# A chunked recurrence's triangular inverse: block-diagonal 128x128 products replaced by pairs of 64x64 products

## The chip, the core and the metric

One core of a Trainium2 chip runs the whole kernel. The metric is device time in microseconds. The engines are PE (matrix products; PEld is its weight load), DVE (vector), ACT (scalar), POOL (here it issues the gathers by index) and SP (here it issues the other transfers).

## The reference

One layer of a streaming encoder for 512 tokens of 1024 features: attention (8 heads) and an RWKV-7 recurrence (8 heads of 64) side by side, then a product-key expert layer with 16384 experts, of which each of 8 heads takes 16 per token.

```python
x = x + jnp.concatenate([y_a, y_b], axis=-1) @ w_o[l]     # y_a attention, y_b recurrence
x = x + peer_ffn(rms_norm(x, g_ffn[l]), ...)
# the recurrence, per head, one token after the other:
sk = jnp.einsum('bhij,bhj->bhi', state, kk_t)
state = (state * w_t[:, :, None, :] - sk[..., None] * (kk_t * a_t)[:, :, None, :]
         + v_t[..., None] * k_t[:, :, None, :])
y = jnp.einsum('bhij,bhj->bhi', state, r_t)
# the expert layer, per block of 128 tokens, after the best 16 per head are found:
act = jax.nn.gelu(jnp.einsum('thkd,td->thk', expert_u[idx], hb), approximate=False)
return jnp.einsum('thk,thkd->td', gate * act, expert_v[idx])
```

The kernel does the recurrence in chunks of 64 tokens. Within a chunk the dependence of a token on those before it is a unit lower triangular 64x64 system per head, and its inverse is needed.

## The kernel before

The 512 tokens are four blocks of 128, and a block is two chunks. Each block goes through five stages: F (norm and projections), R (`rwkv_chunks`: what the chunks need, the inverse among it), M (attention), S (`rwkv_scan`: the recurrence over chunks, whose state update is L756) and B (output projection L792, norm, search L848 and routing of experts, whose last matmuls are L947). A loop at the end of `layer_kernel` steps the stages' generators in turn, by assumed costs and by which stage needs which, and so sets the order in which the code is emitted; from that the framework's scheduler fixes each engine's order. An engine then runs its own list strictly in order and waits at the instruction whose data isn't there.

The expert layer is done in two ways. The tokens of blocks 0 and 3 gather rows of the expert tables: `experts` issues 512 gathers of 128 rows (L978, on POOL), and each is followed by one DVE pass over 128x1024 (L988 for the first table, L991 for the second). Four buffers `ga` take turns. Blocks 1 and 2 go through all experts on PE (`dense`): activations L1103 and L1117, sums `po` L1138 and L1149, with DVE and ACT splitting operands in two parts (L1064, L1063).

The inverse is made by doubling, in levels 1, 2, 4, 8, 16 and 32, with 8 heads side by side in the columns and the two chunks of the block on the two halves of the partitions. X and Y are the inverse so far and its transpose. Each level multiplies the system with X and masks the result (L674, then L683), and two further products give the next X and Y (L690, L692); L702 is the last product. Each product multiplies both chunks at once: the weights are a 128x128 block-diagonal matrix per head, with one chunk in each diagonal block. The block diagonals are `INT` (the system), `YB` and `TB`; `stacked` (L665) fills the latter two on ACT, one half of the partitions at a time. The trace holds two PE records for each of these float32 products. L642 is an earlier product of the same stage, already in 64x64 pieces in quarters of the array, and L730 is one of the scan in one quarter.

The lanes' PSUM banks are counted in `BANKS`: two for R (lane 1) and two for S (lane 4) before.

Of the kernel before, what the change touches and what calls it, by code (L numbers as in the profile page):

```python
# [35 lines left out]
# columns of the packed per-channel vectors  # L36
# [7 lines left out]
# columns of the packed per-feature rows  # L44
# [6 lines left out]
# candidate pairs (a, b) of the two sorted lists that can be among the best 16 sums, in order of a * 16 + b:  # L51
# (a, b) has (a + 1) * (b + 1) - 1 pairs before it that are at least as large
# [3 lines left out]
# lanes of stages: buffers, banks and weight tiles (count, width) of each  # L56
LANE = {"R": 1, "M": 2, "S": 4, "F": 3, "B": 3}
BANKS = {1: 2, 2: 2, 3: 2, 4: 2}
# [5 lines left out]
# blocks whose tokens gather their experts' rows, blocks that go through all experts  # L64
# [4 lines left out]
# dense blocks: gates of HALF * 128 experts at a time, in GBUFS tiles of SUB * 128; activations run AHEAD tiles ahead,  # L69
# FIRST of them before the first gates, KEPT more wait in DRAM  # L70
# [6 lines left out]
def u_whole(e):  # L77
    """float32 products of four passes, where the vector engine has no time to split; else three exact parts"""
    return e < 28 or 47 <= e - AHEAD < 64
# [7 lines left out]
def layer_kernel(ctx: ExitStack, tc: tile.TileContext, x, pos, cvec, rvec, w_mla, w_rwkv, w_uq, w_ukv, lora, g2,  # L87
# [5 lines left out]
    # what the last block's tail needs lies apart: its pools outlive those of the other stages  # L93
# [4 lines left out]
    # the tail takes over the buffers of the second lane  # L98
# [13 lines left out]
    def bank():  # L112
        cnt[0] += 1
        return psums[lane[0]].tile([P, 512], F32, tag=f"ps{lane[0]}", name=f"ps{cnt[0]}", bufs=BANKS[lane[0]])

# [24 lines left out]
    # ---------------------------------------------------------------- constants  # L140
# [65 lines left out]
    # rows (beta s | kappa s), columns (alpha t | rho t)  # L206
# [3 lines left out]
    predl = cst([P, 2, C], "predl", I32)  # L210
    V.tensor_tensor(predl, upp[:, None, :].to_broadcast([P, 2, C]), bdm, op=OP.mult)
    pred1 = cst([P, C], "pred1", I32)
    V.tensor_copy(pred1, lev1t)
    eyebd = med(2, C)
    V.tensor_tensor(eyebd, eye[:, None, :].to_broadcast([P, 2, C]), bdm, op=OP.mult)
    INT = cst([P, H, 2, C], "INT")
    Y1 = cst([P, H, C], "Y1")
    YB = cst([P, H, 2, C], "YB")
    G.memset(YB, 0.0)
    TB = cst([P, H, 2, C], "TB")  # L220
    G.memset(TB, 0.0)
    V.tensor_copy(INT, eyebd[:, None].to_broadcast([P, H, 2, C]))
    V.tensor_copy(Y1, eye[:, None].to_broadcast([P, H, C]))
# [35 lines left out]
    # rotary tables, token-major  # L259
# [50 lines left out]
    def square_sum(src, scr, acc):  # L310
        """the squares go to a tile that is written after them"""
        act(scr, src, AF.Square, accum_out=acc)

    def head_squares(src, n, acc, h0=0):
        """acc[:, h0 + i] = sum of squares of src[:, i, :n]"""
        for i in range(src.shape[1]):
            act(sb([P, QK], "hscr", dt=BF16)[:, :n], src[:, i, :], AF.Square, accum_out=acc[:, h0 + i:h0 + i + 1])

    # ---------------------------------------------------------------- stages
    def norm_in(xt, hT, carry):  # L320
        """channel-major normalized tokens, after the last one of the block before"""
        ss = sb([P, 1], "ss", 2)
        square_sum(xt.rearrange("p (a b) -> p a b", a=KC), hT[:, :, 1:], ss)
        r = rstd(ss, 1, 1.0 / D, EPS, "nx")
        act(xt, xt, AF.Copy, scale=r)
        if carry is None:
            V.memset(hT[:, :, 0:1], 0.0)
        else:
            V.tensor_copy(hT[:, :, 0:1], carry)
        for i in range(2):  # L330
            p = bank()
            for j in range(4):
                nc.tensor.transpose(p[:, j * P:(j + 1) * P], xt[:, (4 * i + j) * P:(4 * i + j + 1) * P], ident)
            for j in range(4):
                act(hT[:, 4 * i + j, 1:P + 1], p[:, j * P:(j + 1) * P], AF.Copy, scale=col("g_mix", 4 * i + j))
            yield
        carry = sb([P, KC, 1], "carry", 2)
        V.tensor_copy(carry, hT[:, :, P:P + 1])
        return carry

    def rwkv_in(b, hT):
        pm = {}
        if b == EARLY:
            # the gather's buffers are idle until the first block's experts are known
            t = [gb([P, D], "ga", GA).rearrange("p (a b) -> p a b", b=P) for _ in range(2)]
            pm = {"k": t[0][:, 0:4], "r": t[0][:, 4:8], "v": t[1][:, 0:4], "x": t[1][:, 4:6]}
# [14 lines left out]
    def mla(b, hT, yT):  # L361
# [31 lines left out]
        # queries  # L393
# [32 lines left out]
        # keys and values  # L426
# [27 lines left out]
        # block-causal attention, four heads at a time  # L454
# [73 lines left out]
    def rwkv_chunks(b, pm):  # L528
# [68 lines left out]
        # bonus weight and gate  # L597
# [8 lines left out]
        # values, token-major  # L606
# [17 lines left out]
        # chunk-local products  # L624
# [12 lines left out]
        # inverse of the unit lower triangular systems: two chunks stacked on the partitions, heads side by side  # L637
        for s in range(2):
            p = bank()
            for j in range(4):  # L640
                for c in range(2):
                    mm(p[c * C:(c + 1) * C, j * C:(j + 1) * C], BK[s * C:(s + 1) * C, j, c, 0, :],  # L642
                       AR[s * C:(s + 1) * C, j, c, 0, :], start=True, stop=True)
            p3 = p[:, :4 * C].rearrange("p (a b) -> p a b", a=4)
            V.copy_predicated(INT[:, s::2], predl[:, None].to_broadcast([P, 4, 2, C]),
                              p3[:, :, None, :].to_broadcast([P, 4, 2, C]))
            V.copy_predicated(Y1[:, s::2], bm(pred1, 4), p3)
            yield
# [13 lines left out]
        def stacked(t, y):  # L662
            for c in range(2):
                q = slice(c * C, (c + 1) * C)
                act(t[q, :, c, :], y[q], AF.Copy)  # L665
# [3 lines left out]
        Y, Yb = Y1, stacked(YB, Y1)  # L669
        X = None  # L670
        for lv in LEVELS:
            t1 = bank()
            for h in range(H):
                mm(t1[:, h * C:(h + 1) * C], INT[:, h].rearrange("p a b -> p (a b)"), eye if X is None else X[:, h, :],  # L674
                   start=True, stop=True)
            t13 = t1.rearrange("p (a b) -> p a b", a=H)
            if lv == 1:
                X = med(H, C)
                V.tensor_tensor(X, t13, bm(lmask[1], H), op=OP.mult)
                yield  # L680
                continue
            t1s = med(H, C)
            V.tensor_tensor(t1s, t13, bm(lmask[lv], H), op=OP.mult)  # L683
            t1b = stacked(TB, t1s)
            if lv == LEVELS[-1]:
                break
            yield
            xp, yp = bank(), bank()
            for h in range(H):
                mm(xp[:, h * C:(h + 1) * C], Yb[:, h].rearrange("p a b -> p (a b)"), t1s[:, h, :], start=True, stop=True)  # L690
            for h in range(H):
                mm(yp[:, h * C:(h + 1) * C], t1b[:, h].rearrange("p a b -> p (a b)"), Y[:, h, :], start=True, stop=True)  # L692
            X = med(H, C)
            act(X, xp.rearrange("p (a b) -> p a b", a=H), AF.Copy)
            yp3 = yp.rearrange("p (a b) -> p a b", a=H)
            Y = med(H, C)
            act(Y, yp3, AF.Copy)
            Yb = stacked(YB, yp3)
            yield
        p = bank()  # L700
        for h in range(H):
            mm(p[:, h * C:(h + 1) * C], t1b[:, h].rearrange("p a b -> p (a b)"), Y[:, h, :], start=True, stop=True)  # L702
        yield
        YF = med(H, C)
        act(YF, p.rearrange("p (a b) -> p a b", a=H), AF.Copy)
        return AR, BKt, MT, UV, YF, wc, bv, sg

    def rwkv_scan(b, AR, BKt, MT, UV, YF, wc, bv, sg, yT):
        # the recurrence over chunks
# [48 lines left out]
        # group norm, bonus, gate  # L758
# [65 lines left out]
    def top16(items):  # L824
        """items: (values, indices, source); the chains of several items interleaved"""
# [11 lines left out]
    def retrieve(bs, h2T):  # L837
        """the best TOPK of both halves' keys, per block"""
# [23 lines left out]
    def route(b, tv, ti):  # L862
        yield
        # the lists of indices as steps: what each rank adds to the one before
# [31 lines left out]
        # rank a of the first list from a candidate's place, rank b of the second from its place within the run  # L896
# [131 lines left out]
    def gate_half(dn, g, parts):  # L1028
        """gates of experts i1 * 128 + i2, i1 in one half: [i2, sub, token, i1 of the SUB]; parts: what takes each run
        of subs"""  # L1030
# [21 lines left out]
    def dense():  # L1052
# [8 lines left out]
        def split(t, hi, lo):  # L1061
            """two parts of a float32 tile that the one-pass products carry whole"""
# [13 lines left out]
        # room for activations in the buffers of the second lane  # L1076
# [14 lines left out]
        def up(e, keep=False):  # L1091
            """activations of the experts of a tile, for all tokens of these blocks"""
# [91 lines left out]
    # stages of the blocks, emitted in the order in which they would run side by side; what runs in one lane shares  # L1184
    # its buffers
# [101 lines left out]
```

## Time and profile before

| | |
|---|---|
| three timed runs | 1781.82, 1783.02, 1790.86 us (median 1783.02) |
| span of the profiled execution | 1781.3 us |
| instructions | 29137 |
| busy: PE, PEld, DVE, ACT, POOL | 1651.5, 1394.3, 1334.4, 932.6, 702.6 us |
| mean granted PE clock | 0.950 of full speed |
| DMA | 520.71 MB, mean 292 GB/s |

The profile gives no other time for the profiled execution than its span. Busy PE counts matmuls whose ends are modelled, so a busy PE is not PE at its peak. The stages of different blocks overlap, so a share over the whole span says little: stretches have to be read.

### The profile page before, as it was taken

To read this page: it belongs to the slowest core of one execution; us is meant where nothing else is said; L and a number is where in the kernel's file an instruction comes from. 1 tells how busy PE (TensorE), PEld (TensorE's weight loads), DVE (VectorE), ACT (ScalarE), POOL (GpSimd) and SP (SyncE) were. 2 spreads that over 40 slices of the span, in tenths; PEclk is the share of its full clock that TensorE was granted. 3 is DMA by queue.
4 is the path that set the end of the run, shared out by engine and by line. 5 is a ranking of instruction groups with operands and counts; after the bars stand their busy time and mean duration, and the time that the engine had idled before them with its cause. 6 is when DMAs were issued, how large, how long until landed. Compare 5 with 4: busy or idle time off the path is not lost. (4 is left out here: it accounts for less than half of the span.)

```text
span 1781.3 us, 29137 instructions
## 1 busy us (share of the span) xinstructions
PE 1651.5 (93%) x10183; PEld 1394.3 (78%) x10183; DVE 1334.4 (75%) x2987; ACT 932.6 (52%) x2465; POOL 702.6 (39%) x562
## 2 busy tenths in 40 slices
PE   7999999998999998788997899999999999999987
PEld 6897799787867987567995577888777778888864
DVE  3412414775586789887789789998887799999898
ACT  5656454644545332367774334444768645445443
POOL 1001100244554444454443253334455446356453
PEclk9998999997697999988999999999989999999999
DMA  7634565596689988789997799998989999999988
GB/s 272 196 122 135 164 233 194 203 337 223 213 309 329 324 321 294 290 283 310 364 331 250 258 359 352 359 355 325 327 312 319 312 343 351 366 318 371 346 293 330
DMA packets 154866, 520.71 MB, mean 292 GB/s; under 512 B 17312, under 2 KB 24096, under 8 KB 154720
## 3 DMA queue, kind: packets, MB, share of 16 engines
q0 software_dynamic: 73728, 268.47, 43.1%
q1 hardware_dynamic: 80992, 250.39, 39.6%
q8 instruction: 80, 1.31, 0.3%
q14 instruction: 66, 0.54, 0.1%
HBM read 508.96 MB, written 9.83 MB: 291 GB/s over the span
## 5 line engine op out<-in xcount | busy, mean ns | idle before, releaser
L978 POOL DMA_INDIRECT ga<-in_expert_v_dram,idx x256 | 352.3, 1376 | 381.7 <-DVE acc L991 285.5
L978 POOL DMA_INDIRECT ga<-in_expert_u_dram,idx x256 | 299.8, 1171 | 372.0 <-DVE ga L988 257.5
L991 DVE SCALAR_TENSOR_TENSOR acc<-ga,dots,acc 128x1024 f32<-128x1024 f32 x256 | 327.9, 1281 | 65.9 <-DMA ga<-in_expert_v_dram,idx 64.9
L988 DVE SCALAR_TENSOR_TENSOR ga<-ga,h 128x1024 f32<-128x1024 f32 x256 | 311.6, 1220 | 52.3 <-DMA ga<-in_expert_u_dram,idx 52.1
L1149 PE MATMUL po<-xh,t 128*128 128x512 f32 x880 | 307.7, 407 | 12.7 <-DVE t L1064 5.7
L1117 PE MATMUL ps<-dh,ul 128*128 128x256 f32 x664 | 191.1, 288 | 7.9 <-DVE ul L1064 7.4
L1149 PEld LDWEIGHTS po<-xh,t 128*128 128x128 f32 x880 | 159.6, 192 | 48.6 <-ACT xh L1063 13.2
L1117 PE MATMUL ps<-dh,uh 128*128 128x256 f32 x664 | 189.8, 286 | 6.5 <-ACT uh L1063 6.5
L1149 PE MATMUL po<-xl,t 128*128 128x512 f32 x440 | 179.6, 408 | 14.6 <-DVE xl L1064 14.2
L1117 PE MATMUL ps<-dl,uh 128*128 128x256 f32 x664 | 187.5, 282 | 0.0
L1063 ACT ACTIVATE xh<-v 128x512 fp32r<-128x512 f32 x220 | 134.6, 626 | 96.4 <-PE po L1149 73.9
L1103 PE MATMUL ps<-t,u 128*128 128x256 f32 x720 | 172.6, 393 | 9.1 <-DMA u<-in_expert_ut_dram 8.8
L1103 PEld LDWEIGHTS ps<-t,u 128*128 128x128 f32 x720 | 138.5, 197 | 32.3 <-issue 6.3
L1064 DVE TENSOR_TENSOR xl<-v,xh 128x512 fp32r<-128x512 f32 x220 | 147.7, 690 | 16.2 <-ACT xh L1063 15.7
L1043 PEld LDWEIGHTS ps<-B,A 128*128 128x128 f32 x1024 | 131.3, 204 | 35.3 <-ACT ge L951 10.6
L1039 ACT ACTIVATE A<-iotap,slots 128x128 f32<-128x128 f32 x512 | 156.1, 395 | 0.0
L1043 PE MATMUL ps<-B,A 128*128 128x64 f32 x1024 | 131.5, 285 | 23.6 <-DVE B L1036 10.4
L1063 ACT ACTIVATE uh<-u 128x512 fp32r<-128x512 f32 x166 | 98.5, 625 | 83.8 <-PE ps L1117 52.0
L1117 PEld LDWEIGHTS ps<-dh,ul 128*128 128x128 f32 x664 | 126.4, 190 | 17.3 <-DVE ul L1064 13.4
L1117 PEld LDWEIGHTS ps<-dh,uh 128*128 128x128 f32 x664 | 126.4, 190 | 17.1 <-ACT uh L1063 10.0
L1117 PEld LDWEIGHTS ps<-dl,uh 128*128 128x128 f32 x664 | 126.4, 190 | 3.5 <-issue 0.7
L848 PE MATMUL ps<-h2T,wst 128*128 128x128 f32 (+1 forms) x768 | 125.1, 318 | 3.1 <-DMA wst<-in_w_pq_dram 3.1
(402 smaller groups left out, 2924.1 us busy)
## 6 DMA issues: line engine op xcount, KB each, us to landing
u<-in_expert_ut_dram SPq DMA_DIRECT2D x128, 512.0 KB, 6.7
v<-in_expert_v_dram SPq DMA_DIRECT2D x128, 512.0 KB, 6.6
wst<-in_w_rwkv_dram SPq DMA_DIRECT2D x56, 512.0 KB, 4.4
wst<-in_w_pq_dram SPq DMA_DIRECT2D x48, 512.0 KB, 6.7
wst<-in_w_o_dram SPq DMA_DIRECT2D x24, 512.0 KB, 5.2
wst<-in_w_mla_dram SPq DMA_DIRECT2D x16, 336.0 KB, 3.9
t<-in_x_dram SPq DMA_DIRECT2D x8, 512.0 KB, 4.6
wst<-in_w_ukv_dram SPq DMA_DIRECT2D x16, 256.0 KB, 3.5
```

What stands on the lines that cost most here:

```text
L848: mm(p[:, :nb * P], w[:, kc, :], h2T[:, kc, :], start=kc == 0, stop=kc == KC - 1)
L978: G.indirect_dma_start(out=t, out_offset=None, in_=table, in_offset=bass.IndirectOffsetOnAxis(ap=idx[:, j:j + 1], axis=0))
L988: V.scalar_tensor_tensor(u, u, 1.0, h2, op0=OP.mult, op1=OP.mult, accum_out=dots[:, j:j + 1])
L991: V.scalar_tensor_tensor(acc, row_of(expert_v, j), dots[:, j:j + 1], acc, op0=OP.mult, op1=OP.add)
L1039: act(A[:, j, :], iotap, AF.Abs, scale=-1.0, bias=i2T[:, t0 + j:t0 + j + 1])
L1043: mm(p[:, j * HALF:(j + 1) * HALF], A[:, j, :], B[:, j, :], start=True, stop=True)
L1063: act(hi, t, AF.Copy)
L1064: V.tensor_tensor(lo, t, hi, op=OP.subtract)
L1103: mm(p, u[:, kc, :], hd[kc // 2][:, kc % 2, :], start=kc == 0, stop=kc == KC - 1)
L1117: mm(p, a[:, k, :], h[:, kc, :], start=kc + i == 0, stop=kc == KC - 1 and i == 2)
L1149: mm(po[i][n], ww[:, i * P:(i + 1) * P], vv, start=e + k == 0, stop=e == P - 1 and k == 2)
```

## The change

The inverse's products no longer use block diagonals. Each product of a level is 16 products of 64x64x64 (8 heads by 2 chunks): chunk 0 takes partitions 0 to 63 of operands and output, chunk 1 takes 64 to 127, so they stand in two different quarters of the array, and each chunk writes its own bank. A mask or a copy is then two instructions over 64 partitions, one for each bank, instead of one over 128. `stacked`, `YB`, `TB` and the zeros around the system in `INT` go. The lanes R and S now share four banks in turn. Stage R gives way to the other stages once more than before (one more `yield`), which moves the order in which code is emitted. The comments that the diff also removes are left out here.

```diff
-BANKS = {1: 2, 2: 2, 3: 2, 4: 2}
+BANKS = {1: 4, 2: 2, 3: 2}
...
-        return psums[lane[0]].tile([P, 512], F32, tag=f"ps{lane[0]}", name=f"ps{cnt[0]}", bufs=BANKS[lane[0]])
+        n = 1 if lane[0] == 4 else lane[0]
+        return psums[n].tile([P, 512], F32, tag=f"ps{n}", name=f"ps{cnt[0]}", bufs=BANKS[n])
...
-            V.copy_predicated(INT[:, s::2], predl[:, None].to_broadcast([P, 4, 2, C]),
-                              p3[:, :, None, :].to_broadcast([P, 4, 2, C]))
+            V.copy_predicated(INT[:, s::2], bm(predl, 4), p3)
...
+        def products(lhs, rhs):
+            ps = [bank(), bank()]
+            for h in range(H):
+                for q, p in zip(halves_, ps):
+                    mm(p[q, h * C:(h + 1) * C], lhs[q, h, :], rhs[q, h, :] if len(rhs.shape) == 3 else rhs[q],
+                       start=True, stop=True)
+            return [(q, p[q].rearrange("p (a b) -> p a b", a=H)) for q, p in zip(halves_, ps)]
+        def masked(ps, m):
+            t = med(H, C)
+            for q, p in ps:
+                V.tensor_tensor(t[q], p, bm(m[q], H), op=OP.mult)
             return t
-        Y, Yb = Y1, stacked(YB, Y1)
-        X = None
-        for lv in LEVELS:
-            t1 = bank()
-            for h in range(H):
-                mm(t1[:, h * C:(h + 1) * C], INT[:, h].rearrange("p a b -> p (a b)"), eye if X is None else X[:, h, :],
-                   start=True, stop=True)
...
-            t1s = med(H, C)
-            V.tensor_tensor(t1s, t13, bm(lmask[lv], H), op=OP.mult)
-            t1b = stacked(TB, t1s)
+        Y = Y1
+        X = masked(products(INT, eye), lmask[1])
+        yield
+        for lv in LEVELS[1:]:
+            t1 = masked(products(INT, X), lmask[lv])
+            yield
             if lv == LEVELS[-1]:
                 break
...
+            X = copied(products(Y, t1))
+            Y = copied(products(t1, Y))
+            yield
+        YF = copied(products(t1, Y))
```

The scheduler's order shows what becomes of it. The first place is PE in the inverse of block 2, at level 2, where L674 multiplies the system with X. Before, the eight products stand in pieces between products of the attention (L486, L487, L497, L503) and of the scan:

```order
L674 MATMUL ps_3950<-t_3934,INT 128x64
L354 MATMUL ps_3692<-hT_3144,wst_3690 128x129 x2
L503 MATMUL ps_3685<-vs_3561,t_3649 128x64
L503 MATMUL ps_3685<-vs_3563,t_3649 128x64
L503 MATMUL ps_3685<-t_3369,t_3649 128x64
L354 MATMUL ps_3692<-hT_3144,wst_3690 128x129 x6
L486 MATMUL ps_3703<-t_3557,t_3486 128x128
L486 MATMUL ps_3703<-t_3559,t_3486 128x128
L486 MATMUL ps_3703<-t_3487,t_3486 128x128
L487 MATMUL ps_3703<-kmask,qmask 128x64
L674 MATMUL ps_3950<-t_3934,INT 128x64
```

In the change the same product is L663, with the banks ps_4223 for chunk 0 and ps_4224 for chunk 1 (L492 and L498 are the former L497 and L503):

```order
L663 MATMUL ps_4223<-t_4209,INT 64x64 x8
L498 MATMUL ps_3998<-vs_3746,t_3996 128x64
L498 MATMUL ps_3998<-vs_3748,t_3996 128x64
L498 MATMUL ps_3998<-t_3575,t_3996 128x64
L492 MATMUL ps_4025<-ident,t_3982 128x128 x3
L663 MATMUL ps_4224<-t_4209,INT 64x64 x8
```

Here the eight products of one chunk stand together, with wide products between them and those of the other chunk. Elsewhere the chunks alternate, as in this piece of block 1's inverse, with L934 (formerly L947) of block 0's routing in it:

```order
L663 MATMUL ps_3258<-t_3164,t_3218 64x64
L663 MATMUL ps_3259<-t_3164,t_3218 64x64
L663 MATMUL ps_3258<-t_3164,t_3218 64x64
L663 MATMUL ps_3259<-t_3164,t_3218 64x64
L663 MATMUL ps_3258<-t_3164,t_3218 64x64
L934 LDWEIGHTS identb
L934 MATMUL ps_2941<-t_2896,identb 128x128
L663 MATMUL ps_3259<-t_3164,t_3218 64x64
L663 MATMUL ps_3258<-t_3164,t_3218 64x64
```

A wide product splits the alternating run there. Over the whole program the 960 small products stand in 122 unbroken runs (29, 41, 17 and 35 for blocks 0 to 3); of the 838 neighbours within a run 563 are of different chunks.

The second place is DVE just ahead of the scan of block 2. Before, its first state update (L756) comes with 46 passes of the gather ahead of it (L988 and L991); these are the last rows:

```order
L988 SCALAR_TENSOR_TENSOR ga_14964,dots_14835<-ga_14964,h_14833 128x1024
L511 TENSOR_TENSOR os_4005<-os_4005,rz_4003 128x8
L305 TENSOR_SCALAR onv_4037<-os_4005 128x8
L592 TENSOR_TENSOR t_4656<-WB,pm_3430 128x8x64
L650 COPY wc_5027<-WB 128x8
L991 SCALAR_TENSOR_TENSOR acc_14831<-ga_14967,dots_14835,acc_14831 128x1024
L988 SCALAR_TENSOR_TENSOR ga_14970,dots_14835<-ga_14970,h_14833 128x1024
L514 TENSOR_TENSOR onr_4039<-onr_4039,rz_4003 128x8
L991 SCALAR_TENSOR_TENSOR acc_14831<-ga_14973,dots_14835,acc_14831 128x1024
L756 TENSOR_TENSOR ST_171<-t_4464,ps_4459 64x4x64 x2
```

In the change L756 is L743, and L988 and L991 are L975 and L978:

```order
L978 SCALAR_TENSOR_TENSOR acc_15345<-ga_15535,dots_15349,acc_15345 128x1024
L975 SCALAR_TENSOR_TENSOR ga_15538,dots_15349<-ga_15538,h_15347 128x1024
L546 SCALAR_TENSOR_TENSOR t_4894<-reset,t_4840 128x512
L978 SCALAR_TENSOR_TENSOR acc_15345<-ga_15541,dots_15349,acc_15345 128x1024
L975 SCALAR_TENSOR_TENSOR ga_15544,dots_15349<-ga_15544,h_15347 128x1024
L587 TENSOR_TENSOR t_5088<-WB,pm_3712 128x8x64
L644 COPY wc_5454<-WB 128x8
L978 SCALAR_TENSOR_TENSOR acc_15345<-ga_15547,dots_15349,acc_15345 128x1024
L975 SCALAR_TENSOR_TENSOR ga_15550,dots_15349<-ga_15550,h_15347 128x1024
L978 SCALAR_TENSOR_TENSOR acc_15345<-ga_15553,dots_15349,acc_15345 128x1024
L743 TENSOR_TENSOR ST_165<-t_4886,ps_4881 64x4x64 x2
```

68 passes now stand ahead of that update, 22 more, and from there on the passes keep a lead of 15 to 26 passes over the other vector work, mostly about 20, until they end. The third place is the end of DVE's list. Before, the gather's passes reach to the end, among the splits of the dense layer (L1064) and the last sums (L1181):

```order
L1064 TENSOR_TENSOR xl_14802<-v_14795,xh_14801 128x512
L1064 TENSOR_TENSOR xl_14812<-v_14795,xh_14811 128x512
L991 SCALAR_TENSOR_TENSOR acc_15613<-ga_16385,dots_15617,acc_15613 128x1024
L991 SCALAR_TENSOR_TENSOR acc_15613<-ga_16388,dots_15617,acc_15613 128x1024
L1181 TENSOR_TENSOR xx_14821<-xx_14821,po_7804 128x512
L1181 TENSOR_TENSOR xx_14821<-xx_14821,po_7805 128x512
L991 SCALAR_TENSOR_TENSOR acc_15613<-ga_16391,dots_15617,acc_15613 128x1024
```

In the change (L1051 and L1168 are the former L1064 and L1181) they are done 40 splits before the last one:

```order
L1051 TENSOR_TENSOR xl_15290<-v_15283,xh_15289 128x512
L1051 TENSOR_TENSOR xl_15300<-v_15283,xh_15299 128x512
L1051 TENSOR_TENSOR xl_15316<-v_15309,xh_15315 128x512
L1051 TENSOR_TENSOR xl_15326<-v_15309,xh_15325 128x512
L1168 TENSOR_TENSOR xx_15335<-xx_15335,po_8318 128x512
```

The order of the transfers on SP and of the gathers on POOL stays nearly as it was; POOL loses two memsets, of `YB` and `TB`.

## Rows read from the trace of the kernel before

**Rows 1.** Page, part 1: busy us, share of the span, instructions of each engine.
```profile
PE 1651.5 (93%) x10183; PEld 1394.3 (78%) x10183; DVE 1334.4 (75%) x2987; ACT 932.6 (52%) x2465; POOL 702.6 (39%) x562
```

**Rows 2.** Stretches: length; PE, PEld, DVE, ACT, POOL busy; granted clock, DMA share, GB/s.
```profile
88.00:143.00 55.00, 52.85 (x437) 51.46 (x436) 9.56 (x26) 30.25 (x89) 1.64 (x1) 0.96 0.36 113
...
210.00:316.00 106.00, 103.73 (x846) 97.38 (x845) 36.45 (x208) 48.22 (x136) 2.76 (x3) 1.00 0.65 213
...
385.00:464.00 79.00, 73.50 (x432) 66.73 (x432) 42.05 (x70) 33.09 (x80) 34.84 (x28) 0.73 0.67 219
...
1060.00:1682.00 622.00, 592.76 (x3502) 511.70 (x3501) 561.93 (x886) 344.73 (x804) 299.26 (x225) 0.98 0.93 340
...
1682.00:1781.30 99.30, 81.74 (x378) 59.81 (x376) 85.87 (x118) 39.52 (x78) 48.35 (x32) 0.98 0.89 315
```

**Rows 3.** Timeline of PE, block 0: start, length (us), line, tiles, shape, records.
```profile
93.38 1.90 PE L674 MATMUL ps<-t,INT 128*128 128x64 f32 x16
95.11 0.44 PE L354 MATMUL ps<-hT,wst 128*128 128x129 f32 x2
...
127.08 2.40 PE L354 MATMUL ps<-hT,wst 128*128 128x129 f32 x20
129.31 1.45 PE L690 MATMUL ps<-t,YB 128*128 128x64 f32 x12
```

**Rows 4.** Timeline of PE around the quarter-array products of block 0 (L642).
```profile
78.21 0.45 PE L642 MATMUL ps<-t,t 64*64 64x64 f32 x8
78.59 0.91 PE L723 MATMUL ps<-t,t 128*64 128x64 f32 x12
79.43 0.49 PE L354 MATMUL ps<-hT,wst 128*128 128x129 f32 x2
79.85 0.68 PE L642 MATMUL ps<-t,t 64*64 64x64 f32 x16
80.46 0.49 PE L354 MATMUL ps<-hT,wst 128*128 128x129 f32 x2
80.79 0.39 PE L486 MATMUL ps<-t,t 96*128 96x128 f32 x2
```

**Rows 5.** Timeline of PE: sixteen records in one quarter of the array (L730).
```profile
149.17 1.14 PE L730 MATMUL ps<-t,t 64*64 64x64 f32 x16
150.24 1.16 PE L540 MATMUL ps<-ga,wst 64*128 64x128 f32 x8
```

**Rows 6.** Timeline of PE: products of block 2 while the granted clock is half.
```profile
429.81 3.67 PE L692 MATMUL ps<-t,TB 128*128 128x64 f32 x16
433.28 3.62 PE L674 MATMUL ps<-t,INT 128*128 128x64 f32 x16
```

**Rows 7.** Groups by line, 0 to 700: busy us, mean ns, idle before.
```profile
L665 ACT ACTIVATE TB<-t 64x512 f32<-64x512 f32 x40 | 25.0, 625 | 17.2 <-DVE t L683 16.8
...
L697 ACT ACTIVATE t<-ps 128x512 f32<-128x512 f32 x16 | 9.6, 598 | 12.1 <-PE ps L692 11.9
...
L683 DVE TENSOR_TENSOR t<-ps,lm 128x512 f32<-128x512 f32 x20 | 13.8, 688 | 29.8 <-PE ps L674 29.7
```

**Rows 8.** Gather issues (L978, POOL) in stretches: length, busy (issues), clock, DMA share.
```profile
339.00:385.00 46.00, 16.88 (x16) 1.00 0.95 344
...
428.00:476.00 48.00, 19.64 (x16) 0.50 0.53 169
...
476.00:657.00 181.00, 80.04 (x72) 0.91 0.90 311
...
469.00:489.00 20.00, 12.67 (x10) 0.82 0.75 232
```

**Rows 9.** Timeline of DVE, block 2; in brackets the wait ahead of it.
```profile
455.52 0.56 DVE L488 TENSOR_REDUCE mx<-ps 128x1 f32<-128x384 f32 x1 [8.03 <-PE ps L487]
...
476.50 0.84 DVE L756 TENSOR_TENSOR ST<-t,ps 64x256 f32<-64x256 f32 x2
```

**Rows 10.** Waits from 1682 to the end: total us, times, longest.
```profile
ACT xh L1063 <- PE po L1149: 28.9, 29, 3.3
```

More of the change, by code (lines that the diff above doesn't have):

```diff
@@ L209, in layer_kernel @@
     V.tensor_tensor(mmask[:, 1, :], upp, eye, op=OP.add)
-    predl = cst([P, 2, C], "predl", I32)
-    V.tensor_tensor(predl, upp[:, None, :].to_broadcast([P, 2, C]), bdm, op=OP.mult)
+    predl = cst([P, C], "predl", I32)
+    V.tensor_copy(predl, upp)
     pred1 = cst([P, C], "pred1", I32)
     V.tensor_copy(pred1, lev1t)
-    eyebd = med(2, C)
-    V.tensor_tensor(eyebd, eye[:, None, :].to_broadcast([P, 2, C]), bdm, op=OP.mult)
-    INT = cst([P, H, 2, C], "INT")
+    INT = cst([P, H, C], "INT")
     Y1 = cst([P, H, C], "Y1")
[L218 to L223, printed above, removed]
+    for t in (INT, Y1):
+        V.tensor_copy(t, eye[:, None].to_broadcast([P, H, C]))
     reset = cst([P, 8, C], "reset", BF16)
@@ L660, in rwkv_chunks @@
             BKt.append(t)
[L662 to L665, printed above, removed]
+        halves_ = [slice(c * C, (c + 1) * C) for c in range(2)]
+        def products(lhs, rhs):
[5 more added lines that the diff above has]
+            return [(q, p[q].rearrange("p (a b) -> p a b", a=H)) for q, p in zip(halves_, ps)]
@@ L666, in stacked, with copied @@
+        def masked(ps, m):
+            t = med(H, C)
+            for q, p in ps:
+                V.tensor_tensor(t[q], p, bm(m[q], H), op=OP.mult)
+            return t
+        def copied(ps):
+            t = med(H, C)
+            for q, p in ps:
+                act(t[q], p, AF.Copy)
             return t
         yield
-        Y, Yb = Y1, stacked(YB, Y1)
-        X = None
-        for lv in LEVELS:
-            t1 = bank()
-            for h in range(H):
-                mm(t1[:, h * C:(h + 1) * C], INT[:, h].rearrange("p a b -> p (a b)"), eye if X is None else X[:, h, :],
-                   start=True, stop=True)
[L676 to L681, printed above, removed]
-            t1s = med(H, C)
-            V.tensor_tensor(t1s, t13, bm(lmask[lv], H), op=OP.mult)
-            t1b = stacked(TB, t1s)
+        Y = Y1
@@ L685, in rwkv_chunks @@
+        X = masked(products(INT, eye), lmask[1])
[3 more added lines that the diff above has]
+            yield
             if lv == LEVELS[-1]:
                 break
+            X = copied(products(Y, t1))
+            Y = copied(products(t1, Y))
             yield
-            xp, yp = bank(), bank()
-            for h in range(H):
-                mm(xp[:, h * C:(h + 1) * C], Yb[:, h].rearrange("p a b -> p (a b)"), t1s[:, h, :], start=True, stop=True)
@@ L691, in rwkv_chunks @@
[L691 to L702, printed above, removed]
+        YF = copied(products(t1, Y))
@@ L703, in rwkv_chunks @@
         yield
-        YF = med(H, C)
-        act(YF, p.rearrange("p (a b) -> p a b", a=H), AF.Copy)
         return AR, BKt, MT, UV, YF, wc, bv, sg
```

## The prediction

> **What bounds the kernel now.** I read the page first: PE is busy 93% of the span, DVE 75% [rows 1]. Then the stretches, because the change sits in the first 660 us alone. While blocks 0 and 1 have their inverse, PE has no gap (52.85 of 55 us, 103.73 of 106), so there a microsecond of PE work is a microsecond of time. Block 2's stretch, 385 to 464, is another place: the granted clock is 0.73 in the mean, PE is busy 73.5 of 79 us, and DVE stands idle 37 of 79. From 1060 to 1682 PE is busy 592.76 of 622 us and DVE 561.93; the last 99 us hold 81.74 of PE [rows 2]. At the end it is ACT that waits for PE's sums, 28.9 us in total [rows 10]. So the dense part and the tail are PE's; the change doesn't touch their work. It can gain or lose only by when they start, and by the gather's passes that stand among DVE's work.
>
> **PE, the products themselves.** A wide product's records follow each other at 0.108 us: sixteen from 93.38 to 95.11 [rows 3]. The 480 products have 960 records, so 103.7 us at full clock. In block 2 at half clock (1.2 GHz) the pace is 0.217 (429.81 to 433.28) [rows 6]; I take it that both kinds slow alike.
>
> The new products don't exist in this trace in their two diagonal quarters. L642 is the nearest: 64x64 pieces that alternate between two quarters. A run of eight records takes 0.38 us to the next matmul, a run of sixteen 0.61, so eight more cost 0.23 (0.029 each), and 0.15 is a fixed part [rows 4]. In one quarter alone sixteen take 1.07; less the fixed 0.15 that is 0.058 each [rows 5]. So alternating halves the price, and a run of one chunk does not. Walking the new order with these two paces (a quarter takes a record each 0.058, the two quarters beside each other where neighbours change chunk, which 563 of 838 do) gives 82.7 us for the 1920 records. The ends are 55.7 (all alternate) and 111.4 (none).
>
> Each run also pays for the change of shape. L354's pace is 0.111 (twenty records, 127.08 to 129.31) [rows 3], yet the two L354 records between L723 and L642 take 0.42 instead of 0.22, and the two behind L642 0.33 [rows 4]. I put 0.1 to going in and 0.1 to coming back, and with the fixed 0.15 a run costs 0.35. 122 runs make 42.7. Sum: 82.7 + 42.7 = 125.4 against 103.7, so PE has 21.7 us more to do, not less. For blocks 0 and 1 (70 runs) it is 40.3 + 24.5 = 64.8 against 51.8, or +13; for blocks 2 and 3, +9. The bounds: -21 if the fixed part is hidden by the other quarter's work, +50 if nothing overlaps. I stay at +22, as both parts of it are read from the same shape in the same stage.
>
> The Trainium skill, TensorEngine Tiling (Array Packing), section Tiling Modes, says two things that pull apart here. Tiles load and multiply in parallel, which agrees with 0.029 against 0.058. And changing the tiling mode, not only the tile, drains the engine, which agrees with the longer gaps at both ends of L642. By the first alone the sum would be -21 us of PE or better, by both +22.
>
> **ACT and DVE.** ACT loses 80 half copies of `stacked`, 0.625 us each in the row of `TB`, and 36 full ones at 0.598; it gets 72 halves [rows 7]. A half costs no less than a full one there, so 71.5 becomes about 45: 27 us off an engine that is busy 52% [rows 1]. I count nothing for it, since L692 comes behind L690 on PE and `TB` was filled meanwhile. DVE's 24 masks at 0.688 [rows 7] become 48. By the same observation a half costs as much as a full one: +16.5 us, less some 3 us for the smaller predicated copies. DVE has room in the first half, but in each level the second mask lies in the chain, 0.69 us by 6 levels, 4 us a block. Against it, where the chunks alternate, the product ahead of it is done sooner by 16 x 0.108 less 32 x 0.029, which is 0.8. These two cancel; both ends are 4 us a block.
>
> **Where the order moves things.** Ahead of the first routing matmul of block 0 (L947) stood all 240 wide products of blocks 0 and 1; now it is 445 of 480 small ones. They cost 445 x 0.086 + 62 runs x 0.35 = 60 us against 52: +8. But 37 products of attention, scan and block 2 have gone behind it, 74 records at 0.111 or more: -8. So the gather starts at 339 us as before. The bounds are -13 (no fixed part) and +8.
>
> Then comes the largest term. 46 passes stood ahead of block 2's first state update, which starts at 476.50 [rows 9]; now it is 68, and DVE takes them strictly in order. What does a pass cost? The gathers went at 16 in 46 us from 339, 16 in 48 from 428, 72 in 181 from 476, but 10 in 20 from 469 [rows 8]. The slow stretches hold waits of DVE for PE, such as 8.03 us ahead of 455.52 [rows 9], and the gathers queue behind them. The new passes stand beside each other with no such wait between, so I price the 22 at the fastest row, 2.0 us: 44 us. Of that the 37 us in which DVE stood idle from 385 to 464 can hide most, so the update comes 7 us later. The bounds are -6 (PE's chain in this half-clocked stretch gets shorter and all 44 are hidden) and +44 (nothing is). Queued behind the update is the scan of block 2, then the back stages of blocks 1 to 3, and then the dense part.
>
> **After that.** The passes among the other vector work are as many as before, since the lead stays about 20. Block 3's inverse costs PE 7 us more (20.8 + 35 x 0.35 = 33 against 26) in a stretch where others have work for PE; I take +2 (0 to 7). At the end the last 40 splits are free of passes. PE is idle for 17.6 us of the last 99 [rows 2], about 9 of them behind the last sum, so at most 8.6 can go; with ACT waiting for PE there I take -5 (0 to -9).
>
> **Sum:** 0 + 7 + 2 - 5 = +4 on the 1781.3 of the profiled execution. The median of the timed runs lies 1.7 above that, so 1787 us, no change that a measurement tells (about 0.5%, 9 us, is what it can).
>
> **Rivals.** *Faster.* The fixed part of a run is hidden. Then PE's work falls by 21 us, 11 of it in the stretches where PE has no gap, the gather starts 13 us sooner, the state update comes 6 us sooner instead of 7 later, the end gains its full 9: -13 - 6 - 9 = -28, so about 1755. For it speaks that PE is the bound in the front; against it the two gaps on each side of L642. By the skill's rule of parallel tiles this is the outcome. The chance is 0.30.
>
> *Slower.* The gathers don't go at 2.0 us. At the 2.5 us of the stretch from 476 the 22 passes cost 55 us, and as the other 46 keep the pace that they had, the update comes 18 us late plus what PE's +13 adds where it has no gap: +31 - 5 + 2 = +28, about 1811. At 3.0 it would be near 1820. It decides as soon as a gather takes more than 2.2 us there: 22 x 2.2 is 48, 11 above the 37 that hide it. For it speaks that three of the four rows are slower, against it that DMA is busy only 0.53 from 428 to 476 [rows 8]. The chance is 0.34.
>
> *The quarters don't overlap* because the scheduler set eight and eight, as in block 2: PE +50 us in all. Half of it in blocks 0 and 1 would come through, and the time is again near 1810; I count it within the slower case.
>
> **How the numbers follow.** No measurable change 0.36, with 1774 to 1792 for it; faster 0.30; slower 0.34. To leave 2 in 10 outside, the range reaches to the faster rival and a little past the slower one: 1755 to 1818.
>
> **What would show it.** L663's records at 0.029 where chunks alternate and 0.058 where they don't, and 0.2 us ahead of and behind each run. The first gather near 339, and the first L743 of block 2 near 484 with 68 passes ahead of it. In the dense part the same share of PE, and an end without gathers. I am wrong if small products cost no gap at a change of shape, if the gathers of block 0 start well off 339, or if the lead of the passes makes the dense part itself quicker or slower.

## The result, and the profile after

The change made the kernel slower: 1804.22 us in the median of 4 runs (1803.23 to 1807.16), against 1782.42 of the kernel before on the same chip (4 runs, 1772.57 to 1790.86). The ratio is 1.0126, with a 95% interval of 1.0082 to 1.0170. The profiled execution spans 1802.4 us. Busy times on its page, and the same stretches as in [rows 2]; the last one is longer, as the end comes later:

```profile
PE 1641.7 (91%) x11143; PEld 1366.5 (76%) x11143; DVE 1355.6 (75%) x3010; ACT 908.2 (50%) x2421; POOL 692.5 (38%) x560
```

```profile
88.00:143.00 55.00, 55.00 (x686) 46.95 (x683) 11.36 (x28) 27.82 (x88) 1.65 (x1) 1.00 0.47 141
210.00:316.00 106.00, 98.97 (x1027) 86.47 (x1025) 48.74 (x269) 38.81 (x118) 1.65 (x1) 0.94 0.46 152
385.00:464.00 79.00, 69.69 (x687) 58.76 (x687) 58.33 (x93) 30.66 (x80) 39.60 (x35) 0.76 0.81 269
...
1060.00:1682.00 622.00, 586.49 (x3392) 501.02 (x3391) 551.44 (x858) 337.69 (x788) 301.20 (x223) 0.97 0.92 333
1682.00:1802.40 120.40, 108.74 (x583) 91.16 (x581) 92.25 (x135) 54.18 (x106) 29.17 (x19) 0.98 0.74 258
```

PE is busy 9.8 us less than before [rows 1], DVE 21.2 us more. From 1060 to 1682 both do less in the same time (PE 592.76 to 586.49, DVE 561.93 to 551.44), so the dense part comes late. The timeline of PE shows the new products (L663) at the forecast paces, in block 0 and then in block 2:

```profile
103.42 0.43 PE L482 MATMUL ps<-kmask,qmask 1*128 1x64 f32 x2
103.78 0.68 PE L663 MATMUL ps<-t,INT 64*64 64x64 f32 x16
104.39 0.38 PE L349 MATMUL ps<-hT,wst 128*128 128x129 f32 x1
...
408.11 1.14 PE L663 MATMUL ps<-t,INT 64*64 64x64 f32 x16
409.18 0.66 PE L498 MATMUL ps<-vs,t 128*128 128x64 f32 x4
```

Sixteen records of alternating chunks take 0.61 us to the next matmul, as L642 did [rows 4]; sixteen of one chunk take 1.07, as L730 did [rows 5]. Now the masks (L670) and copies (L676), grouped by line (busy us, mean ns, idle before):

```profile
L670 DVE TENSOR_TENSOR t<-ps,lm 64x512 f32<-64x512 f32 x48 | 33.0, 687 | 12.2 <-PE ps L663 11.2
```

```profile
L676 ACT ACTIVATE t<-ps 64x512 f32<-64x512 f32 x72 | 42.5, 590 | 44.4 <-PE ps L663 39.3 <-remote 2.4 <-PE ps L498 0.8
```

Half a mask costs 687 ns, a whole one cost 688 [rows 7]; the 48 cost 16.5 us more than 24 would. Last, block 2, from the end of its inverse to its first state update (L743, formerly L756). First PE in the kernel before, then PE and DVE in the change:

```profile
461.74 1.06 PE L702 MATMUL ps<-t,TB 128*128 128x64 f32 x4
462.73 2.07 PE L538 MATMUL ps<-tw,wst 64*128 64x128 f32 x8
...
468.21 1.96 PE L730 MATMUL ps<-t,t 64*64 64x64 f32 x16
```

```profile
462.51 1.81 PE L663 MATMUL ps<-t,INT 64*64 64x64 f32 x31
470.62 3.27 PE L663 MATMUL ps<-t,t 64*64 64x64 f32 x32 [6.30 <-DVE t L670]
473.82 1.64 PE L533 MATMUL ps<-tw,wst 64*128 64x128 f32 x6
...
488.81 1.14 PE L717 MATMUL ps<-t,t 64*64 64x64 f32 x16
```

```profile
468.52 1.23 DVE L975 SCALAR_TENSOR_TENSOR ga<-ga,h 128x1024 f32<-128x1024 f32 x1
469.67 0.08 DVE L975 DVE_READ_ACCUMULATOR ga<-ga,h 128x1 f32 x1
469.79 1.41 DVE L670 TENSOR_TENSOR t<-ps,lm 64x512 f32<-64x512 f32 x2
```

Then ACT and PE ahead of the update, and the update on DVE, all in the change:

```profile
491.61 0.63 ACT L549 ACTIVATE WB<-t 128x512 f32<-128x512 f32 x1 [5.62 <-DVE t L546]
...
496.40 1.28 ACT L595 ACTIVATE pm<-pm,cv 128x128 f32<-128x128 f32 x4 [3.12 <-DVE t L587]
497.58 0.57 ACT L719 ACTIVATE t<-ps 64x512 f32<-64x512 f32 x1
```

```profile
498.21 0.69 PE L727 MATMUL ps<-t,t 128*64 128x64 f32 x4 [7.90 <-ACT t L719]
```

```profile
503.29 0.85 DVE L743 TENSOR_TENSOR ST<-t,ps 64x256 f32<-64x256 f32 x2 [0.71 <-ACT t L739]
```

The update is 27 us later than in [rows 9]. Of these, 11 are there when the inverse ends, for the next product starts at 473.82 and not at 462.73: PE waits 6.30 us for the last two masks (L670), which on DVE stand behind passes. Another 9.5 go to other products that PE's list now has between the inverse and the scan's L717 (formerly L730). The last 6 lie between L717 and the update. There the update doesn't wait for passes itself. ACT does: it stands 5.62 and 3.12 us at instructions of block 3's stage R (L549, L595), whose data DVE makes behind passes (L546, L587); the scan's copy L719 is queued behind them, and PE waits 7.90 us for it.

### The profile page after: what moved, and what is told of

Read it like the earlier page. It is cut to its first block, busy times and chain, and to the rows that moved or that the text cites. A ratio compares the mean times of both kernels' runs of the same rounds, so it can differ in the third digit from the quotient of the medians.

```text
span 1802.4 us, 31074 instructions
## 1 busy us (share of the span) xinstructions
PE 1641.7 (91%) x11143; PEld 1366.5 (76%) x11143; DVE 1355.6 (75%) x3010; ACT 908.2 (50%) x2421; POOL 692.5 (38%) x560
## 5 line engine op out<-in xcount | busy, mean ns | idle before, releaser
L965 POOL DMA_INDIRECT ga<-in_expert_u_dram,idx x256 | 292.0, 1141 | 367.3 <-DVE ga L975 231.1
L978 DVE SCALAR_TENSOR_TENSOR acc<-ga,dots,acc 128x1024 f32<-128x1024 f32 x256 | 327.7, 1280 | 67.8 <-DMA ga<-in_expert_v_dram,idx 65.1
L975 DVE SCALAR_TENSOR_TENSOR ga<-ga,h 128x1024 f32<-128x1024 f32 x256 | 311.9, 1221 | 61.2 <-DMA ga<-in_expert_u_dram,idx 56.6
L1051 DVE TENSOR_TENSOR xl<-v,xh 128x512 fp32r<-128x512 f32 x220 | 149.5, 688 | 41.3 <-ACT xh L1050 38.9
L1104 PEld LDWEIGHTS ps<-dh,ul 128*128 128x128 f32 x664 | 127.6, 192 | 21.2 <-DVE ul L1051 16.9
```

The source lines that it names most:

```text
L965: G.indirect_dma_start(out=t, out_offset=None, in_=table, in_offset=bass.IndirectOffsetOnAxis(ap=idx[:, j:j + 1], axis=0))
L975: V.scalar_tensor_tensor(u, u, 1.0, h2, op0=OP.mult, op1=OP.mult, accum_out=dots[:, j:j + 1])
L978: V.scalar_tensor_tensor(acc, row_of(expert_v, j), dots[:, j:j + 1], acc, op0=OP.mult, op1=OP.add)
L1051: V.tensor_tensor(lo, t, hi, op=OP.subtract)
L1104: mm(p, a[:, k, :], h[:, kc, :], start=kc + i == 0, stop=kc == KC - 1 and i == 2)
```

## The experiments

Theory A: the loss comes from the order, from the passes ahead of block 2's scan and block 3's stage R. Theory B: it comes from PE's price for runs of small products. Theory C, first named for the runs with fewer passes ahead: passes that aren't done in front are only paid at another time. Theory D came last: it comes from the two banks, which double the masks and copies. Ratios are to the kernel before on the same chip, with 95% intervals. The edits are shown shortened.

**46 passes ahead in the change.** The edit gives later passes an order edge, no wait:

```diff
+                    held(V.scalar_tensor_tensor(u, u, 1.0, h2, ...))   # and the pass over the second table
+    def held(i):
+        passes.append(i.ins)
+        if len(passes) > 46: tc.add_manual_dep(i.ins, update.name, NoSync)
```

> The changed kernel, only that the 47th and every later gather pass is issued on DVE behind block 2's first state update, so 46 passes stand ahead of it as in the kernel before, not 68. If the passes ahead of block 2's scan cost the time (theory A), the update comes near 480 us instead of 503, and the time falls by about 20 us, to some 1784. If PE's dearer products cost it (theory B: 22 us more of PE work, 13 of them where PE has no gap), the update may come earlier but the end stays within 5 us of the 1804 of the change.

Measured: 1.0102 (1.0062 to 1.0142), not to be told from the change. The update came at 489.50. The chain that ended last shows where the passes went; first the change, then this kernel:

```profile
PE 14%; DVE 1%; ACT 0%; issue 0%; DMA 0%; DVEq 0%; ACTq 0%
```

```profile
PE 54%; DVE 17%; DMA 16%; issue 6%; ACT 3%; POOL 3%; SPq 0%; DVEq 0%; POOLq 0%; ACTq 0%
```

In the change this chain holds no gather, and the last gather is issued 59 us before the end; here DMA and POOL are back in it, and the last gather comes 20 us before the end. Passes held back in front came back at the end.

**68 passes ahead in the kernel before.** The same edge the other way round.

```diff
+        if len(passes) == 68: tc.add_manual_dep(update, i.ins.name, NoSync)
```

> The kernel before with its wide products, only that block 2's first state update is issued on DVE behind the 68th gather pass instead of the 46th. Theory A: the update comes 20 to 27 us later than 476.5 and the time rises by about 20 us, to some 1803, though no product was changed. Theory B: the time stays within 5 us of the 1782 of the kernel before.

Measured: 1.0243 (1.0193 to 1.0294), and the update came at 545.17. So the order alone can cost as much as the whole loss and more. But it is a harsher order than the change's: forced there, the 68th pass had to be waited for.

**Shared banks alone, in the kernel before.**

```diff
-BANKS = {1: 2, 2: 2, 3: 2, 4: 2}
+BANKS = {1: 4, 2: 2, 3: 2}
+        n = 1 if lane[0] == 4 else lane[0]
```

> The kernel before with one part of the change alone: the lanes R and S share four banks; products, masks and copies stay wide. The scheduler then sets 77 passes ahead of block 2's first state update, more than in the change (68). Theory A: the update comes 30 us or more after 476.5 and the time is 1804 or more, so that the banks alone make the loss. Theory B: 1782, or a few us less because the scan and the inverse no longer wait for each other's banks.

Measured: 1.0240 (1.0204 to 1.0277), the update at 512.07, with wide products. This part of the change does harm, and by the order that the scheduler makes of it: in another order, below, the same banks cost nothing that can be told (1.0019).

**Own banks for R and S, in the change.** The same lines the other way round.

> The changed kernel with two banks each for the lanes R and S, as before; the quarter products stay. The scheduler sets 59 passes ahead of block 2's first state update, halfway between the kernel before (46) and the change (68). Theory A: the update comes near 490 us and the time is some 1793. Theory B: 1804, or more, as each pair of products now needs both banks of its lane.

Measured: 1.0149 (1.0108 to 1.0189). Without the shared banks the loss is not smaller. That alone doesn't clear them, since each pair of products now takes both banks of its lane; but the run with one bank below keeps them and has no loss that can be told.

**Three holds, with shared and with own banks.** Order edges at three places of DVE, as in the first experiment.

```diff
+    HOLD = [(41, scan instruction of block 3's R), (46, block 2's update), (60, block 3's predicated copy)]
```

> The changed kernel with the passes held at three places of DVE's order where the kernel before has as many ahead: the 42nd and later behind the first scan instruction of block 3's stage R, the 47th and later behind block 2's first state update, the 61st and later behind block 3's last predicated copy. Holding at the update alone gave 1.0102 of the time before, and block 3's predicated copies still came at 560 us instead of 513, with PE idle for 18 of the 40 us ahead of 540. Theory A, wider: the passes ahead of both stages cost the time; then block 3's inverse starts by 540 and the ratio falls to 1.003 or less. Theory B, PE's dearer products: the ratio stays at 1.010 or more.

> The changed kernel with two banks each for the lanes R and S, as before, and the same three holds, so that of the change nearly the quarter products alone are left. With own banks and no hold it was 1.0149. Theory A: 1.003 or less, and the products as such cost nothing that can be measured. Theory B: PE's 13 us more in the front and 9 in the rest come through, 1.008 to 1.012.

Measured: 1.0069 (1.0035 to 1.0102) with shared banks, 1.0149 (1.0112 to 1.0186) with own. Block 3's inverse began at 553.9 and 560.5 (before at 524.9), so the holds didn't give the order of before. Theory A gets at most half of the loss in the one, nothing in the other.

**Fewer passes ahead.** `HOLD` with 25, 30 and 44.

> The kernel before with its wide products, with 16 passes fewer ahead of the same three places (25, 30 and 44 instead of 41, 46 and 60). Theory A in its plain form, fewer is better: block 2's update comes some 15 us sooner than 476.5 and the ratio is near 0.992. Rival C, the passes are only paid at another time: the gathers already end with the kernel before, so 16 passes more at the end cost what the front gains, and the ratio is 1.000 or up to 1.010.

> The kernel of the run with own banks and three holds, with 25, 30 and 44 passes ahead instead of 41, 46 and 60. Theory A, plain: faster than that run by some 0.8%. Rival C: as that run, or up to 1% slower, with the last gather no more than 15 us ahead of the end.

Measured: 1.0145 (1.0118 to 1.0171) and 1.0320 (1.0288 to 1.0351). Plain A, fewer is better, has fallen. From 1060 on, the wide kernel with 30 ahead shows why; the columns are those of [rows 2]:

```profile
1060.00:1682.00 622.00, 587.07 (x3379) 503.77 (x3378) 551.72 (x860) 336.89 (x784) 300.09 (x223) 0.96 0.92 335
1682.00:1807.00 125.00, 100.91 (x499) 78.06 (x498) 112.53 (x157) 48.65 (x96) 60.96 (x46) 0.95 0.91 329
```

DVE works 112.53 of the last 125 us, while POOL still issues 46 gathers. DVE's passes are work that must lie somewhere: too many ahead keep the scan waiting, too few stand at the end.

**Unbroken runs.** The scheduler places a small product before others that are ready.

```diff
+            with tc.high_priority(1000):
                 for h in range(H):
                     for q, p in zip(halves_, ps):
                         mm(p[q, h * C:(h + 1) * C], ...)
```

> The changed kernel with the small products emitted at a higher priority for the scheduler, so that wide products no longer stand between them: 46 unbroken runs instead of 122, nearly all with alternating chunks. By the paces found, PE's inverse then costs 1920 x 0.029 = 56 us and 46 x 0.35 = 16, 72 in all, against 125 in the change and 104 of the wide products. The order of the passes comes close to the kernel before: 47 ahead of block 2's first state update, 65 ahead of block 3's predicated copies (before 46 and 60; change 68 and 87). Theory B, PE's price: 50 us less of PE work, of which more than half shows: a ratio of 0.985 or less. Theory A, the passes alone: about 1.000. If it is above 1.010, neither the passes nor the price of a run is the cause.

> The control to the last one: the kernel before with shared banks and the same higher priority for its wide products; 40 passes stand ahead of block 2's first state update and 61 ahead of block 3's predicated copies. PE's inverse costs 104 us as before. Theory A: with the passes back near 46 and 60 the loss of the shared banks (1.024) is gone, 1.000 to 1.005. Theory B: the wide products cost what they cost before, 1.000, and the run with unbroken small products is 25 to 30 us faster than this one. If the priority as such makes the gain, both kernels gain alike.

Measured: 1.0056 (1.0030 to 1.0083) for the small products, 1.0019 (0.9994 to 1.0045) for the wide ones with shared banks. The runs did what was forecast (a whole product, 32 records, 1.09 us to the next matmul):

```profile
80.12 0.71 PE L349 MATMUL ps<-hT,wst 128*128 128x129 f32 x4
80.76 1.15 PE L664 MATMUL ps<-t,INT 64*64 64x64 f32 x32
81.85 0.33 PE L492 MATMUL ps<-ident,t 128*128 128x128 f32 x1
```

And still this kernel is no faster than its control. With a cheap PE and few passes ahead neither B nor A was left for it; what it still had, and the control had not, was each mask and each copy out of a bank twice (the control has the copies of `stacked` instead).

**One bank for both chunks.** With unbroken runs, and then alone.

```diff
-            ps = [bank(), bank()]
+            p = bank()                      # each chunk its own half of the partitions
...
-            for q, p in ps:
-                V.tensor_tensor(t[q], p, bm(m[q], H), op=OP.mult)
+            V.tensor_tensor(t, p, bm(m, H), op=OP.mult)     # copies on ACT likewise
```

> As the run with unbroken small products, but both chunks of a product write one bank, each its own half of the partitions, so that a mask or a copy is one instruction over 128 partitions again (24 masks and 36 copies instead of 48 and 72). 42 runs; 49 and 67 passes ahead at the two places. If the two banks are what lets the quarters work side by side, the pace of L663 rises from 0.029 to 0.058 and PE's inverse costs 56 us more. If not, the pace stays at 0.029, each level is shorter by a mask of 0.69 us, and the ratio is that of the last but one or up to 0.5% lower.

> The changed kernel with one part undone: both chunks of a product write one bank, each its half of the partitions, so that a mask or a copy is one instruction over 128 partitions again (24 masks and 36 copies, not 48 and 72). No priority and no holds: the small products stand in 125 broken runs (change 122), and 70 and 95 passes stand ahead of block 2's first state update and block 3's predicated copies (change 68 and 87). Theory D, the doubled masks and copies (24 x 0.69 = 16.5 us of DVE, 36 x 0.6 = 21.6 us of ACT, and one of each in every level's chain) make the loss: the ratio falls from 1.0126 to 1.000, give or take 0.004. Theory A, the passes: 1.013 or more. Theory B, PE's price for each run: 1.010 to 1.014, since the runs are as many.

Measured: 0.9900 (0.9866 to 0.9933) with unbroken runs, 1764.62 us against 1780.31 and so faster than both kernels; 1.0017 (0.9988 to 1.0045) alone. The first kernel also lacks the added `yield`. Alone, the two places had 70 and 95 passes ahead and PE 125 runs, more than the change in both, and the loss is gone, though block 2's update came no sooner than at 500.6. Masks, copies and the largest group of products, in the run with one bank alone:

```profile
L669 DVE TENSOR_TENSOR t<-ps,lm 128x512 f32<-128x512 f32 x24 | 16.5, 688 | 8.3 <-PE ps L663 8.3
```

```profile
L674 ACT ACTIVATE t<-ps 128x512 f32<-128x512 f32 x36 | 21.4, 599 | 43.4 <-PE ps L663 43.1
```

```profile
L663 PE MATMUL ps<-t,t 64*64 64x64 f32 x896 | 44.7, 242 | 14.3 <-ACT t L512 7.9 <-DVE t L669 6.4
```

The same group in the change:

```profile
L663 PE MATMUL ps<-t,t 64*64 64x64 f32 x896 | 55.8, 250 | 20.6 <-DVE t L670 15.4 <-DVE top L820 5.2
```

DVE and ACT have 16.5 and 21.1 us less to do, and PE's records too are quicker. With two banks the halves of an operand come one mask after the other, so the scheduler may set eight products of one chunk and then eight of the other, at the one-quarter pace; with one mask all sixteen are ready at once. In the change's alternating run at 103.78 the records start in pairs 0.007 us apart, in the run of one chunk at 408.11 singly, 0.058 apart. Of all 1920 small records 624 start within 0.025 us of the one before in the change, and 880 with one bank, so more of them run side by side there. The pages of the two one-bank kernels, unbroken first:

```profile
PE 1601.9 (91%) x11143; PEld 1339.2 (76%) x11143; DVE 1334.2 (75%) x2986; ACT 887.2 (50%) x2385; POOL 717.6 (41%) x560
```

```profile
PE 1622.9 (91%) x11143; PEld 1342.9 (75%) x11143; DVE 1336.1 (75%) x2986; ACT 886.5 (50%) x2385; POOL 713.1 (40%) x560
```

Against the kernel before, the second has PE 28.6 us less busy [rows 1] and takes the same time. So small products alone bring nothing that can be told even so; with the priority PE has 49.6 us less and the time is 1.0% shorter.

The six ratios side by side:

| products | order left to the scheduler | products at a higher priority |
|---|---|---|
| small, two banks, two masks | 1.0126 (the change) | 1.0056 |
| small, one bank, one mask | 1.0017 | 0.9900 |
| wide, shared banks | 1.0240 | 1.0019 |

Down a column, one bank takes off 1.1% and 1.6% (in the second the `yield` goes too). Across, the priority takes off 0.7, 1.2 and 2.2%. It can't be put down to the price of a run, since the wide products gain most from it: what it moves is the order.

How two banks cost this the runs don't show, and the traces speak against the nearest reading, a longer chain in each level. These are the times from the first product of a block's inverse to its last, in us:

| | block 0 | block 1 | block 2 | block 3 |
|---|---|---|---|---|
| before | 53.0 | 104.4 | 77.6 | 131.7 |
| the change | 53.0 | 101.6 | 72.7 | 151.8 |
| one bank | 51.8 | 97.6 | 86.7 | 127.8 |
| two banks, priority | 48.8 | 53.8 | 49.2 | 81.4 |
| one bank, priority | 47.4 | 53.4 | 50.4 | 80.7 |

With the priority the inverses take the same with two banks as with one, and the last mask starts at 560.3 and 560.8. The first split of the dense part then starts at 954.8 against 929.9, so that loss isn't in the inverse's own chain and shows up behind it. Without the priority block 3's inverse is 24 us longer with two banks, yet one bank is the later at the first split (964.4 against 958.5 in the change), level at the hundredth (1139.5 and 1140.9) and 19 us ahead at the 401st (1657.1 and 1676.3). Most of this comes in one stretch; first the change, then one bank, in the columns of [rows 2]:

```profile
1250.00:1460.00 210.00, 191.74 (x983) 154.56 (x983) 166.14 (x240) 141.54 (x389) 109.62 (x84) 0.91 0.87 304
```

```profile
1250.00:1460.00 210.00, 197.55 (x1072) 162.42 (x1071) 173.32 (x253) 146.31 (x399) 107.66 (x85) 0.96 0.89 310
```

No inverse is left there. The change has fewer records done, more idle time on PE and a lower granted clock (0.91 against 0.96). With one bank the scheduler also made another order, and a product holds one bank where it held two; no run separates these from the doubled masks and copies.

## Why the prediction came out as it did

1804 lies within the range, but "no measurable change" was wrong: it was slower, with nearly the size of the slower rival (1811), but not by that rival's mechanism. So that the range held was luck, as far as the mechanism goes.

- **The paces of PE held** (0.61 and 1.07 for sixteen records), and so did the gaps around a run (0.20 us into it in the median of 95 runs at full clock, 0.15 out of it); the sum made of them didn't show. I forecast 21.7 us more of PE work, and PE's busy time fell by 9.8. The mis-sized term is the wide products. From each record's start to the next one's, idle time taken out, they take 124.9 us in the kernel before, where I had put 103.7, and 71.0 of it in blocks 2 and 3, where I had put half of the 103.7. The small ones take 108.7 in the change; my sum, without the 0.2 outside each run, was 101.0. I had priced both kinds at full clock, and part of the inverse runs at half clock, other parts in each kernel. That sum was no base for a term. Nor is a microsecond of PE work one of time: with one bank PE had 28.6 us less, for the same time.
- **"DVE has room in the first half" is the step that failed, as far as the runs show.** The size of the work was right (+16.5 us forecast, 33.0 against 16.5 measured); counting the second bank, with its second masks and copies, at nothing was wrong. Undoing it took the ratio from 1.0126 to 1.0017, about 19 us. "These two cancel" held: with 48 masks the inverses of blocks 0 to 2 took no longer than before (block 3's 20 us longer), and with the priority none took over 1.4 us longer than with 24. The way by which the 19 us arise stays open between DVE's and ACT's time, PE's lost overlap, the banks held and the order. That a mask in front displaces a pass, which is then done among the dense work's splits, isn't shown: by 600 us the change has 105 passes done and one bank 111 (with the priority 112 and 116), but by 960 us 242 and 240 (242 and 247), and the kernel before only 226.
- **The gather's start** was to stay at 339 us; it came at 325.5, the bound of -13 that I had tied to hidden run costs. It came with the shared banks and not with the products: with wide products and shared banks it came at 325.4, with small products and own banks at 339.0.
- **The update of block 2** was forecast 7 us late and came 27 late. The price of a pass held. The gather issues of the change ahead of the update, in the columns of [rows 8], go at 2.0 and 1.9 us each:

```profile
425.00:473.00 48.00, 28.44 (x24) 0.61 0.80 262
473.00:503.30 30.30, 17.64 (x16) 0.81 0.94 340
```

  So the slower rival's condition (over 2.2) wasn't met, and its time came out nearly right for another reason. Of the 37 us in which DVE stood idle from 385 to 464 only 16 were used (58.33 busy against 42.05). I had named DVE's queue ahead of the update alone; the passes acted through the inverse's last masks and through ACT's queue behind block 3's stage R, and 9.5 us lay in PE's own order. And as a term of the sum it was no good: bringing the update forward by 14 us changed the time by nothing that can be told.
- **The end** gained more than the 5 us put down: in the profiled executions DVE's 401st split (L1051, formerly L1064) starts at 1676.3 against 1642.4, 34 us late, and the span ends 21 late. So 13 came back, in an end whose last 49 us hold no passes.

By the Trainium skill, TensorEngine Tiling (Array Packing), section PSUM Bottleneck, tiling speeds up PE but not the evacuation of its sums, which should be vectorized across tiles in one bank. The runs agree: a half cost 687 ns and a whole 688, and one bank took off 1.1%. That rule, which I hadn't weighed, spoke against the change; that the evacuation's time is what cost the 1.1% isn't shown.

## What to carry to other kernels

Splitting an output over two banks doubles the instructions that empty it; where a half costs as much as a whole, try first to keep the outputs of neighbouring quarters in one bank and empty them together, which here was 1.1% and 1.6% faster. Don't count work at nothing because its engine has idle time in that stretch: here undoing it changed the time hundreds of us later, by a way that no run shows. Where a scheduler fixes the order, run each part of a change alone, since a change in the number of banks or a priority moved this kernel by 2%.

## What the runs showed of the hardware

Two quarters on the diagonal of the array (different rows and columns) can write the two halves of one bank side by side. In the unbroken run with one bank a product of 32 records takes 1.08 us to the next matmul, as it took 1.09 with two banks, and not twice the 1.07 that sixteen records in one quarter take:

```profile
80.13 0.71 PE L349 MATMUL ps<-hT,wst 128*128 128x129 f32 x4
80.78 1.15 PE L664 MATMUL ps<-t,INT 64*64 64x64 f32 x32
81.86 0.33 PE L492 MATMUL ps<-ident,t 128*128 128x128 f32 x1
```

The Trainium skill, TensorEngine Tiling (Array Packing), section Gotcha 1: PSUM Pressure, says that different row tiles can't access the same bank at once. Here they are different column tiles too, and the pace shows no cost.
